# Block products' sums seeded in the accumulator banks instead of added from SBUF, in a hybrid three-branch trunk

## The chip, the core and the metric

The kernel runs on one core of a Trainium2 chip. The metric is device microseconds from the start to the end of the program; smaller is better. The profile names the engines PE (TensorE matmuls), PEld (TensorE weight loads), DVE (VectorE), ACT (ScalarE), POOL (GpSimd) and SP (SyncE, which issues most of the DMAs). "L452" is line 452 of the kernel's file.

## What is computed

A decoder trunk of two layers over 256 tokens of width 2048. Each layer normalises its input, projects it with one wide matrix into everything that three token mixers need (sparse attention, a convolution module, stick-breaking attention), and adds the gated sum of the three, projected once more, to its input:

```python
def hybrid_layer(x, norm_w, w_in, conv_w, conv_b, cln_w, cln_b, w_a_out, w_b_out, w_c_out, w_out, cos, sin, top_k):
    h = rms_norm(x, norm_w)
    proj = h @ w_in
    (qa, ka, va, za, qi, ki, wi, ub, zb, qc, kc, vc, zc, gates) = jnp.split(proj, split_points(), axis=-1)
    ...
    y_a = (dsa_attention(qa, ka, va, qi, ki, wi, top_k) * jax.nn.silu(za)) @ w_a_out
    y_b = (conformer_conv(ub, conv_w, conv_b, cln_w, cln_b) * jax.nn.silu(zb)) @ w_b_out
    y_c = (stick_breaking_attention(qc, kc, vc) * jax.nn.silu(zc)) @ w_c_out
    g = jax.nn.sigmoid(gates).reshape(b, s, N_BRANCH, D_MODEL)
    merged = g[:, :, 0] * y_a + g[:, :, 1] * y_b + g[:, :, 2] * y_c
    return x + merged @ w_out
```

All arrays are float32. The change concerns the merge gates of the second and third branch (`g[:, :, 1]`, `g[:, :, 2]`, each 2048 columns of `proj`) and half of the output projection `merged @ w_out`.

## The kernel before

**Products.** Weights come from HBM in units of 256 rows by 512 columns (512 KB), one DMA each on SP's queue. A unit is split into a rounded part (`wh`, or `ph`), made by an ACT cast at line 254, and a remainder (`wl`, `pl`), made by a DVE subtraction at line 258. The activations are split likewise, and each product is the sum of three: part by part, remainder by part, part by remainder. One matmul takes 128 rows and 512 columns; for one unit and one block of 128 tokens that is six matmuls, four with `wh` and two with `wl`, all recorded at line 268.

**The stage.** After the first branch, `run` (from line 520 on) works off one list of units per layer: the remaining gate columns, the branch projections and the output projection. It loads a unit 7 places ahead, casts and subtracts it 3 places ahead, issues its matmuls, and runs the unit's `now` actions behind them. `wh` and `wl` have three buffers each, and every fourth unit uses a buffer of its own (`ph`, `pl`). DVE and SP keep the order of the program; a scheduler places the rows of PE and ACT.

**Block products.** `seven` (from line 439 on) takes a pair of 512-column chunks and half of the 16 row blocks. Tokens, rows and columns are halved, and in place of eight block products it does seven, on sums of blocks of the weights (built by DVE, or by accumulating DMAs of POOL) and of the activations (`hs`, `sums`). There are five pairs in a layer: four of gate chunks, `(b, j)` = (2,0), (2,2), (1,0), (1,2), and one of the output projection. Each pair has four accumulator banks, called X and W (the two token blocks of one chunk) and Z and Y (of the other). The products run in the order P1, P7, P5, P6, P3, P2, P4, each as two half units; the `woven` list places these halves between the ordinary units by a position each, and `fetches` says at which unit the blocks that stay in SBUF are loaded. The other half of the rows is done by ordinary units (`gs`, and for the projection `stretch`), which add to the same banks. A bank's first matmul clears it; the function `opens` records which one that is.

**Sums of products.** Some products belong to more than one of the four results. Before, ACT copies P1 out of X (line 512) and DVE makes three combinations of it with Y and Z while these banks still grow (`combine`, line 452, four instructions per pair), in SBUF (`keep`): U1, U2 and R5. When the ordinary units have finished a bank, its combination is added: for gates in the function `gates` (line 1431) ahead of the sigmoid (line 1433), for the output projection in `arrive`, by the second addition (line 1508) behind that of the residual (line 1506). In layer 0, `leave` then squares the new residual and passes it on through `turned` to the next layer: DVE transposes (line 297), a store by POOL (line 300), a load back (line 306), and a scaling on DVE (line 666).

Four accumulator banks serve the pairs (`bk`, one tile each, taken anew by every pair), and four more, as two double tiles, serve the ordinary products (`acc`).

## Time and profile before

| | |
|---|---|
| median of 3 runs | 1995.35 us (1995.05 to 1995.38) |
| profiled execution | 1996.11 us |
| span of its profile | 1994.3 us |
| mean granted TensorE clock | 0.999 |
| DMA traffic | 472.19 MB, mean 237 GB/s |
| q1, hardware DMA queue | 389.25 MB, 61.5% of 16 engines' time |

The span runs from the first to the last instruction in the profile; the execution's own time has 1.81 us around it. In the chain of work that ended last, PE has 96%, DVE, DMA and issue 1% each. The profile gives one page of totals, and its trace can be asked for waits (who waited for whom, how long and how often), groups of equal instructions, windows of time, and the instructions of a stretch one after the other. In a timeline row the first number is the start in us, the second the duration; `x4` joins four like instructions that follow each other, and what stands in brackets is the idle time of that engine before it, with what ended it.

### The profile page before, as it was taken

Reading aid. Unit: us, or ns where it says so; the run is one execution under the profiler, and the core shown is the slowest. Engines: PE = TensorE matmul, PEld = TensorE weight load, DVE = VectorE, ACT = ScalarE, POOL = GpSimd, SP = SyncE. Lnnn points to the kernel's source line nnn. Section 1 sums busy time; section 2 is a strip of 40 time slices with the busy share of each in tenths; the row PEclk is TensorE's granted clock in tenths of the full one; section 3 lists DMA queues with packets and bytes.
Section 4 is the critical chain, followed back from the end, with each engine's and each line's share of the span. In section 5 each row is a group of like instructions: output and inputs, shape, how many; then the busy total and the mean of one; then the engine's idle time right before and its main releaser. Section 6 shows DMA issues by size and latency. Waiting matters only on the chain.

```text
span 1994.3 us, 26127 instructions
## 1 busy us (share of the span) xinstructions
PE 1983.5 (99%) x9266; PEld 1665.3 (84%) x9266; DVE 1643.4 (82%) x1855; ACT 1335.3 (67%) x1815; POOL 219.8 (11%) x324
## 2 busy tenths in 40 slices
PE   9999999999999999999999999999999999999998
PEld 8889888888888888888888988888888888888886
DVE  8767998878898878798785789988788978788997
ACT  7656667779866555565566576677888675555654
POOL 0111012100011100022111111121000110001120
PEclk9999999999999999999999999999999999999999
DMA  7788679866577887888977886788566778888994
GB/s 275 233 285 259 186 226 286 247 190 186 169 217 225 254 257 227 244 258 275 301 253 230 280 257 178 237 285 249 173 179 182 221 225 254 244 250 246 274 292 162
DMA packets 239938, 472.19 MB, mean 237 GB/s; under 512 B 17536, under 2 KB 30336, under 8 KB 239680
## 3 DMA queue, kind: packets, MB, share of 16 engines
q1 hardware_dynamic: 208768, 389.25, 61.5%
q0 software_dynamic: 29376, 78.14, 15.4%
q10 hardware_dynamic: 1664, 3.15, 0.4%
q8 instruction: 72, 1.18, 0.2%
q14 instruction: 58, 0.48, 0.1%
HBM read 437.70 MB, written 32.77 MB: 236 GB/s over the span
## 4 chain that ended last, share of the span: by engine, by line
PE 96%; DVE 1%; DMA 1%; issue 1%; POOL 0%; ACT 0%; DVEq 0%; POOLq 0%; ACTq 0%
PE acc L268 71%; PE bk L268 19%; PE mm L268 3%; DMA zy<-z 1%; PE mm L1089 1%; DVE wl L258 1%; PE mm L1180 0%; DMA z<-zt 0%; PE mm L1286 0%; PE mm L1232 0%; PE mm L1148 0%; DMA raw<-in_w_c_dram 0%; POOL z L300 0%; PE mm L844 0%; PE mm L1262 0%
## 5 line engine op out<-in xcount | busy, mean ns | idle before, releaser
L268 PE MATMUL acc<-wh,s 128*128 128x512 f32 (+1 forms) x4152 | 1028.0, 389 | 1.3 <-DVE s L1376 1.3
L258 DVE TENSOR_TENSOR wl<-raw,wh 128x1024 fp32r<-128x1024 f32 (+1 forms) x636 | 769.6, 1213 | 224.6 <-ACT wh L254 220.6
L254 ACT CAST wh<-raw 128x1024 fp32r<-128x1024 f32 (+1 forms) x635 | 660.9, 1044 | 377.7 <-PE acc L268 223.8
L268 PEld LDWEIGHTS acc<-wh,s 128*128 128x128 f32 x4152 | 772.1, 188 | 152.8 <-issue 2.0
L268 PE MATMUL acc<-wl,s 128*128 128x512 f32 (+1 forms) x1884 | 500.9, 388 | 0.6 <-DVE wl L258 0.6
L268 PEld LDWEIGHTS acc<-wl,s 128*128 128x128 f32 x1884 | 353.2, 188 | 72.0 <-DVE wl L258 1.0
L652 ACT ACTIVATE s<-yT,cst 128x256 f32<-128x256 f32 x480 | 209.7, 500 | 44.6 <-DVE s L929 43.6
L268 PE MATMUL bk<-wh,s 128*128 128x512 f32 x896 | 230.5, 389 | 0.0
L300 POOL DMA_DIRECT2D z<-zt x180 | 106.0, 602 | 1038.9 <-DVE zt L297 1037.9
L268 PEld LDWEIGHTS bk<-wh,s 128*128 128x128 f32 x896 | 167.9, 188 | 35.5 <-DVE t L452 0.9
L929 DVE TENSOR_TENSOR s<-s,s 128x1024 f32<-128x1024 f32 x120 | 146.3, 1219 | 0.0
L268 PE MATMUL bk<-wl,s 128*128 128x512 f32 x448 | 128.7, 389 | 0.0
L254 ACT CAST wh<-s 128x1024 fp32r<-128x1024 f32 x63 | 66.3, 1053 | 50.0 <-PE bk L268 24.2
L268 PEld LDWEIGHTS bk<-wl,s 128*128 128x128 f32 x448 | 84.1, 188 | 17.5
L258 DVE TENSOR_TENSOR wl<-s,wh 128x1024 fp32r<-128x1024 f32 x63 | 76.9, 1221 | 19.7 <-ACT wh L254 19.0
L268 PE MATMUL bk<-ph,s 128*128 128x512 f32 x304 | 78.5, 389 | 0.0
L496 POOL DMA_DIRECT2D s<-in_w_in_dram x32 | 38.7, 1209 | 323.0 <-DVE wl L258 149.6
L254 ACT CAST ph<-raw 128x1024 fp32r<-128x1024 f32 x47 | 49.5, 1054 | 32.7 <-PE bk L268 23.0
L268 PEld LDWEIGHTS mm<-s,wl 128*128 128x128 f32 x512 | 66.9, 191 | 5.0
L268 PEld LDWEIGHTS bk<-ph,s 128*128 128x128 f32 x304 | 57.1, 188 | 11.9
L306 POOL DMA_DIRECT2D zy<-z x50 | 36.5, 730 | 268.9 <-DMA z<-zt 79.6
L268 PE MATMUL mm<-s,wl 128*128 128x192 f32 x512 | 66.0, 271 | 0.0
(297 smaller groups left out, 1611.6 us busy)
## 6 DMA issues: line engine op xcount, KB each, us to landing
raw<-in_w_in_dram SPq DMA_DIRECT2D x519, 512.0 KB, 4.4
raw<-in_w_out_dram SPq DMA_DIRECT2D x56, 512.0 KB, 6.2
zy<-z POOLq DMA_DIRECT2D x48, 512.0 KB, 5.4
z<-zt POOLq DMA_DIRECT2D x172, 128.0 KB, 4.3
raw<-in_w_a_dram SPq DMA_DIRECT2D x32, 512.0 KB, 3.8
raw<-in_w_c_dram SPq DMA_DIRECT2D x32, 512.0 KB, 5.7
s<-in_w_in_dram POOLq DMA_DIRECT2D x32, 512.0 KB, 6.7
raw<-in_w_b_dram SPq DMA_DIRECT2D x32, 512.0 KB, 5.9
```

Of the source, the lines that this page charges most:

```text
L254: newest_parts[0] = nc.scalar.copy(u[1], u[0])
L258: newest_parts[1] = sub = nc.vector.tensor_sub(u[2], u[0], u[1].bitcast(F32))
L268: newest[0] = nc.tensor.matmul(o, lhsT, rhs, start=start, stop=stop, skip_group_check=True)
L300: nc.gpsimd.dma_start(z[:, :, :, a, :].rearrange("t b c e -> c (t b) e"), tmp[a * 32:(a + 1) * 32].rearrange("c t b k i -> c (t b) (k i)"))
L306: nc.gpsimd.dma_start(y.rearrange("p (t a) k i -> p t (a k i)", a=4), z.rearrange("t b c a e -> (b c) t (a e)"))
L496: nc.gpsimd.dma_start(held[to, h], block(b, h), accum_op=ALU.add)
L652: nc.scalar.activation(dst[:, i, :], y, AF.Copy, scale=wq)
L929: nc.vector.tensor_add(cs, cs, home(q - 1))
L1089: nc.tensor.matmul(ps[:, q * S:(q + 1) * S], qi[i][:, hd, :], ki[j][:, 0, :], start=n == 0, stop=n == 2)
```

## The change

The combinations are no longer kept in SBUF and added last. They are written into the banks ahead of the products that come later, and those products then accumulate on top. The products' order becomes P1, P2, P5, P6, P7, P3, P4. After P1, ACT copies X to SBUF (`save`); after P5, ACT copies Z, and DVE writes Z less the saved X into Y (`seed`); after P6, ACT copies Y into Z; after P7, DVE writes the saved Z less Y into W. For the pairs with `b == 2` that last difference goes to SBUF (`apart`) and is added ahead of one sigmoid as before. All other sigmoids read the banks, and `arrive` has one addition left. A bank that is seeded counts as opened. In the first pair of a layer an extra matmul opens Y (`fresh`). `banks` hands out the four tiles turned by two from pair to pair, so that X and W of a pair are Z and Y of the one before. The positions in `woven` and `fetches` are new, and so is where the gate units stand among the branch projections (`m`).

```diff
     def halves(tiles):
         return [v[:, i * 512:(i + 1) * 512] for v in tiles for i in range(2)]
-    def quarters(v):
-        v = v.rearrange("p (k a) t -> p k (a t)", a=2)
-        return [v[:, i, :] for i in range(4)]
     def forms(v):
         (a11, a12), (a21, a22) = ([v[:, i * 4:i * 4 + 4, t * P:(t + 1) * P] for i in range(2)] for t in range(NT))
...
         nc.vector.tensor_sub(a11, a11, a22)
         nc.vector.tensor_sub(a12, a12, a11)
-    def seven(w, cols, act, sums, banks, keep, by_transfer, long=()):
+    def seven(w, cols, act, sums, banks, keep, by_transfer, long=(), apart=None, fresh=False):
...
         X, W, Z, Y = range(4)
         held = {}
-        V, U2, U1, R5 = range(4)
-        def combine(op, dst, a, b):
-            dst, a, b = ({"b": banks, "k": keep}[n][0][i] for n, i in (dst, a, b))
-            op(dst, a, b)
+        def save(i, bank):
+            nc.scalar.copy(keep[0][i], banks[0][bank])
+        def seed(bank, a, b):
+            opens(banks[0][bank])
+            if b is None:
+                nc.scalar.copy(banks[0][bank], banks[0][a])
+            else:
+                nc.vector.tensor_sub(banks[0][bank], a(), b())
+        def bank_of(i):
+            return lambda: banks[0][i]
+        def kept(i):
+            return lambda: keep[0][i]
         def block(b, h):
             k, n = (int(i) - 1 for i in b)
...
             def products(u):
                 for i, j in ((0, 0), (1, 0), (0, 1)):
                     for k in range(2):
+                        if fresh and bank == X and opens(banks[0][Y]):
+                            mult(banks[0][Y], part(a, i, k0, 1, ts)[:, 0, :], u[1][:, 0, :], True, False)
                         mm = mult(banks[0][bank], part(a, i, k0 + h * 2 + k, 1, ts)[:, 0, :], u[1 + j][:, k, :],
                                   opens(banks[0][bank]), False)
                 return mm
...
         p1, p2, p4 = (("11", act, 0, 0, X), ("21", act, 4, 0, X), ("11", act, 4, 1, W))
         p5, p6, p3 = (("11", sums, 4, 1, Z), ("11", sums, 0, 0, Y), ("22", sums, 4, 0, Z))
         p7 = ("12", sums, 0, 1, Y)
-        order = [p1, p7, p5, p6, p3, p2, p4]
+        order = [p1, p2, p5, p6, p7, p3, p4]
         subs = [sub(h, *v) for v in order for h in range(2)]
-        P1, P7, P5, P6, P3, P2, P4 = (subs[n:n + 2] for n in range(0, 14, 2))
+        P1, P2, P5, P6, P7, P3, P4 = (subs[n:n + 2] for n in range(0, 14, 2))
         for h in range(2):
             for b, last, at in (("12", P1, P7), ("22", P5, P6), ("21", P6, P4)):
                 if b in by_transfer:
...
                 else:
                     at[h].early = [partial(add, h, "11", b)]
             P7[h].early = [*P7[h].early, partial(add, h, "12", "22")]
-        add_, sub_ = nc.vector.tensor_add, nc.vector.tensor_sub
-        P1[1].now = [lambda: nc.scalar.copy(keep[0][V], banks[0][X])]
-        P7[1].now = [partial(combine, add_, ("k", U1), ("k", V), ("b", Y))]
-        P5[1].now = [partial(combine, sub_, ("k", R5), ("b", Z), ("k", V))]
-        P6[1].now = [partial(combine, sub_, ("k", U1), ("b", Y), ("k", U1)),
-                     partial(combine, sub_, ("k", U2), ("k", V), ("b", Y))]
-        extra = {(0, 1): U2, (1, 0): U1, (1, 1): R5}
-        return fetch, subs, lambda q, t: keep[0][extra[q, t]] if (q, t) in extra else None
+        P1[1].now = [partial(save, 0, X)]
+        P5[1].now = [partial(save, 1, Z), partial(seed, Y, bank_of(Z), kept(0))]
+        P6[1].now = [partial(seed, Z, Y, None)]
+        if apart:
+            P7[1].now = [lambda: nc.vector.tensor_sub(apart(), keep[0][1], banks[0][Y])]
+        else:
+            P7[1].now = [partial(seed, W, kept(1), bank_of(Y))]
+        return fetch, subs
     def run(units, tasks):
...
         for i in (4, 0):
             split_at(hs, i, 4, v[:, i:i + 4, :])
+        turn = [0]
         def banks():
-            return Lazy(1, lambda: [mp[0].tile([P, 512], F32, tag="bk", name=nm("bk")) for _ in range(4)])
+            def make():
+                b = [mp[0].tile([P, 512], F32, tag="bk", name=nm("bk")) for _ in range(4)]
+                turn[0] += 2
+                return b[turn[0] % 4:] + b[:turn[0] % 4]
+            return Lazy(1, make)
         units, woven, fetches = [], [], []
         for b, j in ((2, 0), (2, 2), (1, 0), (1, 2)):
             og, act, wb = O_G + b * D, (gb, gc)[b - 1], (w_b, w_c)[b - 1][layer]
             g_banks, kept = banks(), Lazy(1, lambda: halves([t4(), t4()]))
-            fetch, subs, share = seven(w, (og + (j + 1) * 512, og + j * 512), hx, hs, g_banks, kept, ("12", "21"),
-                                       ("22",) if b == 2 else ())
+            fetch, subs = seven(w, (og + (j + 1) * 512, og + j * 512), hx, hs, g_banks, Lazy(1, lambda: [ev(), ev()]),
+                                ("12", "21"), ("22",) if b == 2 else (),
+                                (lambda kept=kept: kept[0][1]) if b == 2 else None, not units)
             base = len(units)
-            woven += [(base + (2.5 + 0.75 * n if b == 1 else 4.7 + 0.68 * n), u) for n, u in enumerate(subs)]
+            at, step = ((4.1, 0.64), (2.2, 0.8), (-0.3, 0.9), (-2.3, 1.14))[base // 16]
+            woven += [(base + at + step * n, u) for n, u in enumerate(subs)]
             ys, gs = [], []
             for q in (1, 0):
                 def g(q=q, g_banks=g_banks):
...
                 def sg(q=q, kept=kept):
                     return kept[0][q * 2:q * 2 + 2]
-                def gates(b, c, q, g, sg, share):
+                def gates(b, c, g, sg, apart):
                     for t in range(NT):
-                        v, to = g()[t], sg()[t]
-                        if share(q, t) is not None:
-                            nc.vector.tensor_add(to, v, share(q, t))
-                            v = to
-                        nc.scalar.activation(to, v, AF.Sigmoid)
+                        v = g()[t]
+                        if apart and t:
+                            nc.vector.tensor_add(sg()[t], v, sg()[t])
+                            v = sg()[t]
+                        nc.scalar.activation(sg()[t], v, AF.Sigmoid)
                     if b == 1 and c == 3:
                         warm_sqrt()
...
                 c, y = j + 1 - q, Lazy(1, token_accs)
                 gs += [plain(w, og + c * 512, hx, k, g, KD, True) for k in range(KC, KD, 2)]
                 ys.append([plain(wb, c * 512, act, k, partial(y.__getitem__, 0), KC) for k in range(0, KC, 2)])
-                gs[-1].now = [partial(gates, b, c, q, g, sg, share)]
+                gs[-1].now = [partial(gates, b, c, g, sg, b == 2 and not q)]
                 gs[-1].after = [partial(close, b, c, t, y, sg) for t in reversed(range(NT))]
             if j == 0:
                 ys = [[*ys[0][:2], *ys[1][:2]], [*ys[0][2:], *ys[1][2:]]]
                 if b == 1:
                     ys[0][-1].now = [settle]
-            m = 4 + b
+            m = 4 if b == 1 else 6
             units += ys[0] + ys[1] + gs[4:m] + gs[:4] + gs[m:]
-            fetches.append((fetch, (base - 2, base + 1) if b == 1 else (base + 4, base + 6)))
+            fetches.append((fetch, ((4, 6), (17, 19), (28, 31), (42, 45))[base // 16]))
         last = layer == DEPTH - 1
         ssq = small(8).rearrange("p (t j) -> p t j", t=NT)
...
         wo = w_out[layer]
         p0 = 0 if last else 2
         o_banks = banks()
-        fetch, subs, part_of = seven(wo, (p0 * 512 + 512, p0 * 512), mx, sums, o_banks, Lazy(1, lambda: quarters(slot())),
-                                     ("12", "21"))
+        fetch, subs = seven(wo, (p0 * 512 + 512, p0 * 512), mx, sums, o_banks, Lazy(1, lambda: [ev(), ev()]), ("12", "21"))
         acc, xcs, base = {}, {}, len(units)
         def accs(q):
...
             xc = xcs[q]
             for t in range(NT):
                 nc.vector.tensor_add(xc[:, t, :], acc[q][t], xc[:, t, :])
-                if part_of(p0 + 1 - q, t) is not None:
-                    nc.vector.tensor_add(xc[:, t, :], xc[:, t, :], part_of(p0 + 1 - q, t))
         def leave(q):
             xc, c0 = xcs[q], q * 512
```

In rows of the built program's order, a tile has its name and numbers, then what it is made from, the shape, and how many alike follow. Three places matter below.

**P1 to P2, second pair of layer 0.** On PE, where `bk` is a bank of the pair, `acc` a bank of the ordinary products and `s8` the activations; before:

```order
L268 MATMUL bk_1129_6509<-wh_1110_6407,s8_3_87 128x512 x4
L268 MATMUL bk_1129_6509<-wl_1111_6408,s8_3_87 128x512 x2
L268 MATMUL acc_1126_6491<-wh_1114_6429,s8_814_4854 128x512 x8
L268 MATMUL acc_1126_6491<-wl_1115_6430,s8_814_4854 128x512 x4
L268 MATMUL bk_1132_6512<-ph_1117_6447,s8_993_5871 128x512 x4
```

Here P1's second half ends in bank 6509, and P7 follows in another bank, 6512. Now:

```order
L268 MATMUL bk_1124_6472<-ph_1107_6368,s8_3_87 128x512 x4
L268 MATMUL bk_1124_6472<-pl_1108_6369,s8_3_87 128x512 x2
L268 MATMUL acc_1140_6529<-wh_1112_6409,s8_813_4853 128x512 x6
L268 MATMUL bk_1124_6472<-wh_1109_6386,s8_4_88 128x512 x4
L268 MATMUL bk_1124_6472<-wl_1110_6387,s8_4_88 128x512 x2
```

P2 now goes into P1's bank, with six matmuls of an ordinary unit between the two. On ACT, the row that reads the bank in that gap, in the changed order:

```order
L254 CAST wh_1109_6386<-raw_1111_6388 128x1024
L254 CAST wh_1112_6409<-raw_1114_6411 128x1024
L254 CAST wh_1116_6431<-raw_1118_6433 128x1024
L254 CAST ph_1119_6449<-raw_1121_6451 128x1024
L445 COPY ev_1133_6510<-bk_1124_6472 128x512
```

The save stands behind the cast of `ph_1119`.

**P7 to the gate unit, same pair.** On PE before, with P7 already past and P6's bank 6512 followed by other products:

```order
L268 MATMUL bk_1132_6512<-ph_1145_6579,s8_993_5871 128x512 x4
L268 MATMUL bk_1132_6512<-pl_1146_6580,s8_993_5871 128x512 x2
L268 MATMUL bk_1131_6511<-wh_1147_6590,s8_5_89 128x512 x4
L268 MATMUL bk_1131_6511<-wl_1148_6591,s8_5_89 128x512 x2
L268 MATMUL bk_1131_6511<-wh_1150_6609,s8_994_5872 128x512
L268 MATMUL bk_1132_6512<-wh_1147_6590,s8_5_89 128x512 x4
```

Now P7 is what ends in Y (6475), and an ordinary gate unit writes Z (6474) and Y by turns:

```order
L268 MATMUL bk_1127_6475<-wh_1152_6603,s8_993_5871 128x512 x4
L268 MATMUL bk_1127_6475<-wl_1153_6604,s8_993_5871 128x512 x2
L268 MATMUL bk_1126_6474<-wh_1155_6618,s8_5_89 128x512 x4
L268 MATMUL bk_1127_6475<-wh_1155_6618,s8_5_89 128x512 x4
L268 MATMUL bk_1126_6474<-wl_1156_6619,s8_5_89 128x512 x2
```

On DVE, the reads of these banks and what stands around them, before:

```order
L258 TENSOR_TENSOR wl_1151_6610<-long_1113_6426,wh_1150_6609 128x1024
L258 TENSOR_TENSOR wl_1153_6621<-long_1113_6426,wh_1152_6620 128x1024
L452 TENSOR_TENSOR t4_1139_6549<-bk_1132_6512,t4_1139_6549 128x512
L452 TENSOR_TENSOR t4_1138_6548<-t4_1138_6548,bk_1132_6512 128x512
L258 TENSOR_TENSOR pl_1155_6638<-raw_1156_6639,ph_1154_6637 128x1024
```

and now:

```order
L258 TENSOR_TENSOR wl_1156_6619<-raw_1157_6620,wh_1155_6618 128x1024
L258 TENSOR_TENSOR pl_1159_6638<-long_1103_6343,ph_1158_6637 128x1024
L258 TENSOR_TENSOR wl_1161_6648<-raw_1162_6649,wh_1160_6647 128x1024
L523 TENSOR_TENSOR t4_1173_6718<-ev_1134_6511,bk_1127_6475 128x512
L258 TENSOR_TENSOR wl_1164_6662<-long_1103_6343,wh_1163_6661 128x1024
```

Two reads of a bank have become one, with four matmuls between P7's last row and the next write of its bank.

**The end of layer 0's output projection.** On DVE, the rows of `arrive` (`t4` is the residual) and the transposes behind them, before:

```order
L1506 TENSOR_TENSOR t4_1468_8263<-bk_1409_7951,t4_1468_8263 128x512
L1508 TENSOR_TENSOR t4_1468_8263<-t4_1468_8263,s8_1416_7987 128x512
L1506 TENSOR_TENSOR t4_1468_8263<-bk_1410_7952,t4_1468_8263 128x512
L1508 TENSOR_TENSOR t4_1468_8263<-t4_1468_8263,s8_1416_7987 128x512
L258 TENSOR_TENSOR wl_1501_8416<-raw_1502_8417,wh_1500_8415 128x1024
L297 STREAM_TRANSPOSE zt_1507_8497<-t4_1468_8263 128x4x4x32
```

and now:

```order
L1523 TENSOR_TENSOR t4_1477_8262<-bk_1415_7947,t4_1477_8262 128x512
L1523 TENSOR_TENSOR t4_1477_8262<-bk_1416_7948,t4_1477_8262 128x512
L258 TENSOR_TENSOR wl_1510_8416<-raw_1511_8417,wh_1509_8415 128x1024
L297 STREAM_TRANSPOSE zt_1516_8495<-t4_1477_8262 128x4x4x32 x2
L258 TENSOR_TENSOR wl_1533_8577<-raw_1531_8574,wh_1532_8576 128x1024
```

Two additions are gone ahead of these transposes; a third goes with the other chunk of the pair.

## The prediction

> **What bounds the kernel now.** I read the busy shares first, then what TensorE (PE) waits for, then single stretches in order of time. In the profile page's first part each entry is busy time, share of the span, and instructions:
>
> ```profile
> PE 1983.5 (99%) x9266; PEld 1665.3 (84%) x9266; DVE 1643.4 (82%) x1855; ACT 1335.3 (67%) x1815; POOL 219.8 (11%) x324
> ```
>
> PE is busy for all but 10.8 us of the 1994.3-us span. The view of waits (total us, times, longest) lists everything that PE waited for in the whole run, and then, from the view of the weight loads (PEld), the one line that belongs to the code that changes:
>
> ```profile
> PE acc L268 <- DVE s L1376: 1.3, 1, 1.3
> PE mm L844 <- DVE eps L87: 1.1, 1, 1.1
> PE acc L268 <- DVE wl L258: 0.6, 1, 0.6
> ...
> PEld bk L268 <- DVE t L452: 0.9, 4, 0.2
> ```
>
> That is 3.0 us in three waits. Line 844 is the start of the program, line 1376 the passage ahead of the first block pair; both lie ahead of what changes. So the time is the number of matmuls times their pace, and an edit on another engine counts only through PE. The pace, from the timeline (start, duration, engine, line, operation):
>
> ```profile
> 975.90 1.98 PE L268 MATMUL bk<-wh,s 128*128 128x512 f32 x8
> 977.71 1.07 PE L268 MATMUL bk<-wl,s 128*128 128x512 f32 x4
> 978.62 0.39 PE L268 MATMUL bk<-ph,s 128*128 128x512 f32 x1
> ```
>
> Twelve matmuls take 978.62 − 975.90 = 2.72 us, 0.2267 each. To see how much the changed stage loses today I set its length against this pace:
>
> ```profile
> 675.15 1.07 PE L268 MATMUL bk<-wh,s 128*128 128x512 f32 x4
> ...
> 996.30 1.07 PE L268 MATMUL acc<-wh,s 128*128 128x512 f32 x4
> ```
>
> Between these two rows layer 0 issues 1416 matmuls of this form: 1416 × 0.22667 = 320.96 us, and 321.15 passed. The whole stage, pairs and all, loses 0.19 us. **There is nothing there to win**; what the change can do is lose, or alter the few waits elsewhere. The windows (busy time of each engine with its instructions, then granted clock and DMA share) show how near the other engines are: the first pair, and the stretch from the end of the gates into the output projection.
>
> ```profile
> core 0: us, PE busy (x) PEld busy (x) DVE busy (x) ACT busy (x) POOL busy (x), PEclk, DMA share, GB/s
> 667.00:733.00 66.00, 66.00 (x291) 54.50 (x292) 54.22 (x54) 38.21 (x39) 5.98 (x5) 1.00 0.88 272
> 912.00:986.00 74.00, 74.00 (x328) 61.29 (x327) 57.55 (x60) 41.67 (x49) 15.38 (x21) 1.00 0.94 287
> ```
>
> VectorE (DVE) is busy 82% in the first, ScalarE (ACT) 58%. Both have room on average, so what matters is when each single hand-off comes.
>
> **The change, part by part.** The additions that go and those that come have these durations (groups by shape: busy us, mean ns, idle before and its releaser):
>
> ```profile
> L258 DVE TENSOR_TENSOR wl<-raw,wh 128x1024 fp32r<-128x1024 f32 x83 | 100.9, 1220 | 23.4 <-ACT wh L254 22.5
> L254 ACT CAST wh<-raw 128x1024 fp32r<-128x1024 f32 x83 | 87.3, 1053 | 66.8 <-PE bk L268 37.9 <-PE acc L268 15.6 <-DVE raw L470 5.6
> L1379 DVE TENSOR_TENSOR s<-s,t 128x512 f32<-128x512 f32 x16 | 11.1, 692 | 0.6
> ...
> L452 DVE TENSOR_TENSOR t<-bk,t 128x512 f32<-128x512 f32 x8 | 5.5, 687 | 0.0
> ...
> L512 ACT COPY t<-bk 128x512 f32<-128x512 f32 x4 | 2.3, 578 | 0.0
> ```
>
> *Removed adds.* DVE has 46 additions fewer in both layers, 46 × 0.69 = 32 us of its 1643; ACT has 20 copies more, 20 × 0.58 = 12 us of its 1335. PE waited for neither there, so this counts nothing by itself; what hides it is PE's own stream of 321 us per layer.
>
> *Added matmuls.* In the first pair of each layer one extra product opens bank Y. 2 × 0.2267 = **+0.45 us**, straight on the bound engine.
>
> *The four old hand-offs.* Before, PE met DVE's additions at line 452 four times. One of them:
>
> ```profile
> 699.83 0.69 DVE L452 TENSOR_TENSOR t<-bk,t 128x512 f32<-128x512 f32 x1
> 700.43 0.68 DVE L452 TENSOR_TENSOR t<-t,bk 128x512 f32<-128x512 f32 x1
> ...
> 701.16 0.75 PEld L268 LDWEIGHTS bk<-wh,s 128*128 128x128 f32 x4 [0.21 <-DVE t L452]
> 701.21 1.15 PE L268 MATMUL bk<-wh,s 128*128 128x512 f32 x4
> ...
> 702.20 0.62 PE L268 MATMUL bk<-wl,s 128*128 128x512 f32 x2
> ```
>
> The weight load waits 0.21, yet the four matmuls take 702.20 − 701.21 = 0.99 instead of 0.91: 0.08 us lost. Four of these go: **−0.32 us**.
>
> *New hand-offs.* Now a sum must be *in the bank* before the next product of that bank starts, a wait that PE did not have. I counted in the changed order how many matmuls stand between the last product that feeds a sum and the first that needs the bank. P1 to P2 (ACT saves X): 6 in the second pair of a layer, 12 in the others. P5 to P6 (DVE seeds Y): 9 or more. P6 to the next writing of Y (ACT seeds Z from Y): 6 in the fourth pair, 12 or more elsewhere. P7 to the gate product that writes Y again (DVE reads Y): 7, 4, 5, 7 in the first four pairs, many in the last. What each needs: the two additions above follow each other without a pause, so the start costs some 0.05 and the release of PE another 0.05 (701.16 against the addition's end at 700.43 + 0.68 = 701.11), with 0.69 between them: 0.79 us on DVE, 0.68 on ACT. Cover: 4 matmuls are 0.91 us, 5 are 1.13, 6 are 1.36, 7 are 1.59. An idle engine always makes it. Two conditions remain. In the second pair ACT's save stands behind a cast of 1.05 us whose buffer comes free some 0.45 us before P1 ends, so 1.05 − 0.45 + 0.68 = 1.28 of 1.36: just hidden. And the eight with 4 to 7 matmuls stand behind a weight subtraction of 1.22 us on DVE. In the second pair its cast's buffer comes free 10 matmuls (2.27 us) before P7's end, cast and subtraction take 1.05 + 1.22 and two starts of 0.05, 2.37 together: it ends 0.10 us after P7, where 0.91 − 0.79 = 0.12 is what the cover leaves. I charge each of the eight what the old ones lost, 8 × 0.08 = **+0.64 us**. The ends: nothing at all, or a subtraction that has just begun each time, 1.22 + 0.79 = 2.01 us against the cover: 2 × (2.01 − 0.91) + 2 × (2.01 − 1.13) + 4 × (2.01 − 1.59) = 5.64 us for both layers. I stay near the low end, since the nearest row is the hand-off at 701.16.
>
> *Price of a write into a bank.* No row of before has DVE or ACT writing a bank. It is bounded by the nearest rows, below by nothing, above by the operation of twice the width: 1.22 us in place of 0.69 would leave the 4- and 5-matmul covers short by 2 × (1.32 − 0.91) + 2 × (1.32 − 1.13) = 1.20 us, and 1.05 in place of 0.58 on ACT leaves even the 6-matmul gap of the fourth pair covered (1.15 of 1.36). I take the price of a read, 0.69 and 0.58, whose rows have the same width. A page of the Trainium skill bears on this, "Perfetto Trace Analysis", section "Optimizing Scalar/DVE Operations": it gives VectorE some 60 ns of fixed overhead on SBUF and 125 on PSUM. By the groups above DVE's addition with a bank operand takes 687 against 692 without one, so the trace does not show it for reads, and no run here shows it yet for writes; by the page, 0.065 more on each seed would use half of the 0.12 us that the tightest cover leaves, and the sum would stay.
>
> *The layer change.* The third wait above, 0.6 us, hangs on the end of layer 0's output projection. The additions that go there, the chain behind them and the stall:
>
> ```profile
> L1508 DVE TENSOR_TENSOR t<-t,s 128x512 f32<-128x512 f32 x3 | 2.1, 692 | 0.1
> ...
> 1004.40 1.31 DVE zt L297 x2
> ...
> 1007.73 6.31 DMA z<-zt
> ...
> 1014.56 5.43 DMA zy<-z
> ...
> 1020.01 1.23 DVE L666 TENSOR_TENSOR s<-zy,cst 128x1024 f32<-128x1024 f32 x1 [3.18 <-DMA zy<-z]
> ...
> 1022.36 1.22 DVE L258 TENSOR_TENSOR wl<-raw,wh 128x1024 fp32r<-128x1024 f32 x1
> ...
> 1023.63 1.21 PE L268 MATMUL acc<-wl,s 128*128 128x512 f32 x4 [0.59 <-DVE wl L258]
> ```
>
> Transposes, store, load and scaling run as one chain; the scaling holds DVE's weight subtraction to 1022.36 and PE stands 0.59 us for it. In the changed order three additions of line 1508 (2.1 us) no longer stand ahead of these transposes, so the chain comes up to 2.1 us earlier, and 0.59 is all there is to win: **−0.59 us**. If the two DMAs take the gain, it is 0. What is late next is nothing that PE waits for in the page.
>
> *Order, banks, fetches.* The rotation gives the next pair's first banks to the tiles that the last pair left first; the gaps I counted there are 26 matmuls (5.9 us) or more, so releasing costs nothing, and it would cost only if a 0.6-us sigmoid came 5 us late. Transfers keep their number; fetches start at other units. The waits on their landing are ACT's, and one stands near PE:
>
> ```profile
> 931.27 1.05 ACT L254 CAST wh<-raw 128x1024 fp32r<-128x1024 f32 x1 [5.17 <-DMA raw<-in_w_out_dram]
> ...
> 933.74 1.07 PE L268 MATMUL acc<-wh,s 128*128 128x512 f32 x4
> ```
>
> Here the weights were 5.17 us late for ACT; the cast ended at 932.32 and PE took it at 933.74, 1.42 us to spare. I cost this at nothing, since the loads issue in the same order.
>
> **Sum**: 0.45 − 0.32 + 0.64 − 0.59 = +0.18 us. The profiled execution took 1996.11 us (1.81 around the span), 0.76 above the median of 1995.35; since all terms are differences I put them on the median: **1995.5 us**. Its own range goes from 1994.5 (stage losses of 0.36 in both layers and the old and layer-change waits gone, no new ones: 0.45 − 0.36 − 0.32 − 0.59 = −0.82) to 1996.7 (the price bound, 0.18 + 1.20).
>
> **Rivals.**
> 1. *Late seeds (slower).* Each of the eight short hand-offs meets DVE inside a subtraction of 1.22 us. For it: DVE runs in program order, is 82% busy, and the changed order puts a subtraction right ahead of the bank's read; my margin in the second pair is 0.02 us. Against it: the four old hand-offs, squeezed likewise, cost 0.08 each. It decides from the point where that subtraction ends more than 0.12 us after P7. Time: 1995.5 + 5.64 = 2001.1 us. Chance 0.07.
> 2. *Weights late.* The moved fetches push the load at 931.27 back by another 5.17 us: 5.17 − 1.42 = 3.75 us of PE, 1999.3. For it: DMA share 0.94 there. Against: the same bytes in the same queue. Chance 0.05.
> 3. *The layer change keeps its wait*, because the DMAs set it or another subtraction comes first; then that part of the change does nothing: 0.45 − 0.32 + 0.64 = +0.77, 1996.1. For it: 6.31 and 5.43 us of landing against 2.1 us of gain. Chance 0.14.
> 4. *The clock gate.* PE would idle briefly at each new hand-off and fall to half clock: 12 matmuls in 5.44 us instead of 2.72, once for each of the eight short hand-offs, 8 × 2.72 = 21.8 us, 2017.3. Against it, this stall and what followed:
>
> ```profile
> 666.88 2.08 PE L268 MATMUL acc<-wh,s 128*128 128x512 f32 x8 [1.25 <-DVE s L1376]
> ...
> 668.80 1.07 PE L268 MATMUL acc<-wl,s 128*128 128x512 f32 x4
> ```
>
> After 1.25 us of standing still the next 8 matmuls took 1.92 us against 1.81, and the window that begins there has a granted clock of 1.00. Chance 0.01. The rule stands in the Trainium skill, "TensorE: Matmul & The Clock Gate", section "A second HAM failure mode: psum-queue depth-cycling": short idle times between groups that cycle through accumulator banks make the clock fall and rise; by that rule, the trace of before does not agree, as far as its one longer gap shows.
>
> **How the numbers follow.** A measurement of this kernel tells about 0.2% from no change, 4.0 us: the bounds are 1991.4 and 1999.3. The forecast has 0.72, rival 1 0.07, rival 2 0.05, rival 3 0.14, rival 4 0.01, and 0.01 stays for a gain that nothing in the page shows, since all waits of PE together are 3.0 us. Slower: rivals 1 and 4 and, as 1999.3 lies on the bound, half of rival 2: 0.10. Faster: 0.01. Same: 0.89. The range goes from 1994.5 to rival 2's 1999.3, which leaves out rivals 1 and 4 and little more; the late seeds' full bound lies beyond it, the first half of it inside.
>
> **What would show it.** PE's matmuls number two more. In the waits of PE, line 258 is gone and line 1376 still has 1.3 us; weight loads of the banks wait for the seeds (lines 452 and 523 of the changed kernel) some 0.2 us each, about eight times. If a matmul into a bank shows half a microsecond or more behind these lines, rival 1 holds; if PE waits for a cast that waited for a load, rival 2; if 0.6 us remain near 1023, rival 3; a granted clock below 0.99 in a pair is rival 4. The forecast is wrong if the stage's 1416 matmuls and one take over 323 us.

## The result and the profile after

| | before | changed |
|---|---|---|
| median | 1995.2 us (4 runs, 1995.03 to 1995.38) | 2008.47 us (4 runs, 2006.95 to 2009.28) |
| ratio | | 1.0066, 95% interval 1.0048 to 1.0083 |
| profiled execution, span | 1996.11, 1994.3 | 2009.09, 2007.3 |
| mean granted clock | 0.999 | 0.997 |

The change makes the kernel slower by 13 us, 0.66%. The time lies outside the predicted range and on the side that had a chance of 0.10. The first part of the changed kernel's page, then everything that its PE waited for:

```profile
PE 1990.4 (99%) x9268; PEld 1666.3 (83%) x9268; DVE 1615.3 (80%) x1809; ACT 1341.8 (67%) x1835; POOL 219.4 (11%) x324
```

```profile
PE bk L268 <- DVE bk L452: 6.8, 3, 4.1
PE mm L852 <- DVE eps L87: 1.1, 1, 1.1
PE acc L268 <- DVE s L1384: 0.8, 1, 0.8
PE bk L268 <- ACT wh L254: 0.3, 1, 0.3
```

PE has two matmuls more, as forecast. DVE has 28 us of work less (forecast: 32), ACT 6.5 us more (forecast: 12). But PE, which before never stood at a bank of the pairs, now stands 6.8 us for the seed of a bank (line 452), in three places. Starts of the same matmuls in both traces show where the time came from:

| | before | changed | moved by |
|---|---|---|---|
| start of the stage, layer 0 | 666.88 | 666.16 | −0.72 |
| first matmul behind layer 0's last bank | 996.30 | 998.03 | +2.45 since the row above |
| start of the stage, layer 1 | 1656.81 | 1657.62 | −0.92 |
| tail behind layer 1's last bank | 1975.32 | 1988.34 | +12.21 |

That is 13.02 us. The layer change did win what was forecast, and somewhat more: its wait for line 258, 0.59 us, is gone from the list; where the rest of the 0.92 us comes from is not shown. Nearly all of the loss is in the second layer's stage. There PE stands twice, at the seeds of Y in the fourth and in the last pair. In the timeline, the rows behind each stall:

```profile
1865.16 1.87 PE L268 MATMUL bk<-ph,s 128*128 128x512 f32 x4 [2.09 <-DVE bk L452]
...
1867.69 2.53 PE L268 MATMUL acc<-wh,s 128*128 128x512 f32 x8
...
1870.06 1.07 PE L268 MATMUL acc<-wl,s 128*128 128x512 f32 x4
...
1940.14 1.78 PE L268 MATMUL bk<-ph,s 128*128 128x512 f32 x4 [4.06 <-DVE bk L452]
```

From 1865.16 to 1870.06 PE issues 14 matmuls, which take 4.90 us instead of 14 × 0.2267 = 3.17. The windows (clock in the column ahead of the DMA share) say why:

```profile
core 0: us, PE busy (x) PEld busy (x) DVE busy (x) ACT busy (x) POOL busy (x), PEclk, DMA share, GB/s
1865.00:1867.00 2.00, 1.84 (x5) 1.45 (x6) 2.00 (x3) 0.32 (x1) 0.20 (x1) 0.61 1.07 196
1867.00:1869.00 2.00, 2.00 (x7) 1.58 (x6) 1.95 (x3) 1.04 (x1) 0.99 (x1) 0.54 1.04 362
1869.00:1871.00 2.00, 2.00 (x11) 1.64 (x10) 1.92 (x2) 0.70 (x1) 0.00 (x0) 1.00 1.04 248
...
1940.00:1942.00 2.00, 1.86 (x5) 1.54 (x6) 2.00 (x3) 0.43 (x1) 0.48 (x1) 0.63 0.94 288
```

So each long stall costs 1.7 us again, at about half the clock. Of the 12.21 us, 2.09 + 4.06 + 0.27 are stalls, 2 × 1.73 the slow clock, 0.23 the extra product, and 2.1 are left: about 1.5 for the short hand-offs, 0.1 to 0.2 each, and 0.6 because weights of the last pair's P5 came late themselves.

Why the last seed was late stands in DVE's timeline. The products of P5, whose bank the seed reads, were done at 1933.3, and DVE, in order, works without a pause at what stands ahead:

```profile
1931.30 1.23 DVE L258 TENSOR_TENSOR wl<-s,wh 128x1024 fp32r<-128x1024 f32 x1 [6.51 <-ACT wh L254]
1932.44 1.22 DVE L476 TENSOR_TENSOR s<-s,s 128x1024 f32<-128x1024 f32 x1
1933.57 1.22 DVE L258 TENSOR_TENSOR wl<-raw,wh 128x1024 fp32r<-128x1024 f32 x1
1934.85 1.23 DVE L258 TENSOR_TENSOR pl<-s,ph 128x1024 fp32r<-128x1024 f32 x1
1935.99 1.22 DVE L599 TENSOR_TENSOR s<-zy,s 128x1024 fp32r<-128x1024 f32 x1
1937.13 1.22 DVE L476 TENSOR_TENSOR s<-s,s 128x1024 f32<-128x1024 f32 x1
1938.26 1.22 DVE L258 TENSOR_TENSOR wl<-raw,wh 128x1024 fp32r<-128x1024 f32 x1
1939.40 0.69 DVE L452 TENSOR_TENSOR bk<-bk,ev 128x512 f32<-128x512 f32 x1
```

Seven operations, 8.1 us, stand ahead of the seed. The first is the remainder of P5's own weights, the six behind it are for later units. All are late because the first had waited 6.51 us for an ACT cast. That cast waited for an accumulating load of weight blocks. The chain that ended last has it (11.10 us to land), and POOL's timeline says when it was issued:

```profile
1917.72 0.72 POOL L306 DMA_DIRECT2D zy<-z  x1 [8.45 <-DMA z<-zt]
1918.42 0.60 POOL L300 DMA_DIRECT2D z<-t  x1
1919.02 1.26 POOL L504 DMA_DIRECT2D s<-in_w_out_dram  x1
```

```profile
1919.02 11.10 DMA s<-in_w_out_dram
...
1930.21 1.06 ACT wh L254
```

The load stood in POOL's queue behind a load-back that waited 8.45 us for its store. Before, POOL had the two the other way round:

```profile
1909.29 1.24 POOL L496 DMA_DIRECT2D s<-in_w_out_dram  x1 [0.53 <-DVE wl L258]
1910.67 0.72 POOL L306 DMA_DIRECT2D zy<-z  x1
```

In the fourth pair the seed is late by the same road but a smaller cause: ACT stands 2.85 us for a load-back that line 598 scales, and DVE has five operations between its scaling (1856.81) and the seed (1864.41).

### The profile page after: what moved, and what is told of

It reads as the page before. It is cut to its first block, busy times and chain, and to the rows that moved or that the text cites. A ratio compares the mean times of both kernels' runs of the same rounds, so it can differ in the third digit from the quotient of the medians.

```text
span 2007.3 us, 26101 instructions
## 1 busy us (share of the span) xinstructions
PE 1990.4 (99%) x9268; PEld 1666.3 (83%) x9268; DVE 1615.3 (80%) x1809; ACT 1341.8 (67%) x1835; POOL 219.4 (11%) x324
## 4 chain that ended last, share of the span: by engine, by line
PE 94%; DMA 2%; DVE 2%; issue 1%; ACT 1%; POOL 0%; DVEq 0%; ACTq 0%; POOLq 0%
PE acc L268 69%; PE bk L268 19%; PE mm L268 3%; DMA zy<-z 1%; DMA z<-zt 1%; PE mm L1097 1%; DMA s<-in_w_out_dram 1%; DVE wl L258 0%; PE mm L1188 0%; DVE s L476 0%; PE mm L1294 0%; PE mm L1240 0%; PE mm L1156 0%; DVE s L599 0%; PE mm L852 0%
## 5 line engine op out<-in xcount | busy, mean ns | idle before, releaser
L258 DVE TENSOR_TENSOR wl<-raw,wh 128x1024 fp32r<-128x1024 f32 (+1 forms) x630 | 761.9, 1212 | 228.3 <-ACT wh L254 224.7
L268 PE MATMUL bk<-wh,s 128*128 128x512 f32 x905 | 235.4, 391 | 0.9 <-DVE bk L452 0.6
L254 ACT CAST wh<-s 128x1024 fp32r<-128x1024 f32 x71 | 74.6, 1052 | 69.5 <-PE bk L268 51.1
L258 DVE TENSOR_TENSOR wl<-s,wh 128x1024 fp32r<-128x1024 f32 x71 | 86.5, 1220 | 33.7 <-ACT wh L254 33.4
L254 ACT CAST ph<-raw 128x1024 fp32r<-128x1024 f32 x53 | 55.8, 1053 | 49.9 <-PE bk L268 25.2
L258 DVE TENSOR_TENSOR pl<-raw,ph 128x1024 fp32r<-128x1024 f32 x53 | 64.7, 1221 | 14.3 <-ACT ph L254 11.6
```

The lines of the kernel that those rows point to most:

```text
L254: newest_parts[0] = nc.scalar.copy(u[1], u[0])
L258: newest_parts[1] = sub = nc.vector.tensor_sub(u[2], u[0], u[1].bitcast(F32))
L268: newest[0] = nc.tensor.matmul(o, lhsT, rhs, start=start, stop=stop, skip_group_check=True)
```

## The experiments

The theory from these rows, A: DVE and ACT work in order, and fall behind by some us whenever a transfer is late. Before, this was free, because a combination had no deadline. Now a product waits for it. The rival, B: the new places of products and fetches starve the weights, and PE would wait whoever adds the sums.

**1. The old sums in the new places.** Before's kernel with three edits:

```diff
-            woven += [(base + (2.5 + 0.75 * n if b == 1 else 4.7 + 0.68 * n), u) for n, u in enumerate(subs)]
+            at, step = ((4.1, 0.64), (2.2, 0.8), (-0.3, 0.9), (-2.3, 1.14))[base // 16]
+            woven += [(base + at + step * n, u) for n, u in enumerate(subs)]
...
-            m = 4 + b
+            m = 4 if b == 1 else 6
...
-            fetches.append((fetch, (base - 2, base + 1) if b == 1 else (base + 4, base + 6)))
+            fetches.append((fetch, ((4, 6), (17, 19), (28, 31), (42, 45))[base // 16]))
```

> Old sums (combined in SBUF, added last, old product order, no turning of the banks) with the new positions of products, fetches and gate units. Theory A (the seed of Y after P5 is a deadline that the in-order queues of DVE and ACT miss in two pairs of the second layer, and the clock falls after those stalls): no seed, no deadline, 1995.5 us, within 1.5. Theory B (the new positions starve the weights, and PE waits whoever adds the sums): 2004 us or more, with PE waiting for casts or loads in the pairs.

Measured: 1996.85 us against 1996.41 of before in the same runs, ratio 1.0000 (0.9990 to 1.0009). B falls. ACT's timeline, and the waits of PE, show that the lateness itself is there as well:

```profile
1921.66 1.05 ACT L254 CAST wh<-s 128x1024 fp32r<-128x1024 f32 x1 [4.65 <-DMA s<-in_w_out_dram]
```

```profile
PE acc L268 <- DVE s L1376: 1.3, 1, 1.3
PE mm L844 <- DVE eps L87: 1.1, 1, 1.1
PE acc L268 <- DVE wl L258: 0.4, 1, 0.4
PE acc L268 <- ACT ph L254: 0.2, 1, 0.2
```

The same load makes ACT wait 4.65 us at the same place, and no product of a bank waits for anything. The new places make the engines late; it takes the rest of the change to make PE pay. That rest is the seeds together with the new order of products and the turned banks, which this kernel leaves out as well; experiment 10 separates them.

**2. One deadline less.**

```diff
-        P5[1].now = [partial(save, 1, Z), partial(seed, Y, bank_of(Z), kept(0))]
+        P5[1].now = [partial(save, 1, Z)]
```

> The changed kernel without the one subtraction that seeds Y after P5 (its result leaves out that term; P6 then starts Y by itself). A: the waits of PE for it (0.61, 2.09 and 4.06 us) and the two slow stretches behind the longer ones (some 1.7 us each) go: 2008.5 - 6.8 - 3.5 = 1998.2 us, within 1.5. B: 2006 us or more, the stalls stay in the same places with another releaser.

Measured: 2009.05 us, ratio 1.0058 (1.0042 to 1.0075): no gain. A's number was wrong. The timeline shows where the stalls went:

```profile
887.93 1.19 PE L268 MATMUL bk<-wh,s 128*128 128x512 f32 x4 [2.40 <-DVE bk L452]
...
1882.79 2.08 PE L268 MATMUL bk<-wh,s 128*128 128x512 f32 x4 [2.02 <-DVE bk L452]
...
1949.60 1.20 PE L268 MATMUL bk<-ph,s 128*128 128x512 f32 x4 [2.31 <-ACT bk L450]
```

They moved to the next hand-offs of the same pairs: the seed of W after P7, the copy into Z after P6. I read this so: PE's stall at the first deadline is what lets DVE and ACT catch up; without it they stay late and the next deadline collects. A then says that the lag of the queues is what costs, wherever the next deadline stands.

**3. More room between P5 and P6.** In the fourth pairs and the last one of the second layer:

```diff
-            woven += [(base + at + step * n, u) for n, u in enumerate(subs)]
+            woven += [(base + (5.05 + 0.55 * (n - 6) if base == 48 and n in (6, 7) else at + step * n), u)
+                      for n, u in enumerate(subs)]
...
-            woven += [(base + 1.2 + 0.9 * n, u) for n, u in enumerate(subs)]
+            woven += [(base + (7.05 + 0.6 * (n - 6) if n > 5 and n < 10 else 1.2 + 0.9 * n), u)
+                      for n, u in enumerate(subs)]
```

> P6 later by half a unit in the fourth pair of both layers and in the last pair of the second, so that 24 instead of 12 matmuls lie between P5 and P6 there; sums as in the changed kernel. A: the stall of 2.09 us goes, that of 4.06 shrinks by 2.7 to 1.3 and with them the slow stretches: 2008.5 - 2.1 - 2.7 - 3.5 = 2000.2 us, within 2. B: no gain, 2007 or more, since late weights stay as late.

Measured: 2003.41 us, 1.0035 (1.0023 to 1.0047). It gains, but 3 us less than expected. The last pair's 4.06 became 1.22, as worked out; stalls of 0.57, 0.81 and 1.39 us came at the copies into Z, as in experiment 2. No slow clock is left (0.999 for the run).

**4. The last pair half a unit earlier,** so that POOL issues the load first:

```diff
-            woven += [(base + 1.2 + 0.9 * n, u) for n, u in enumerate(subs)]
+            woven += [(base + 0.7 + 0.9 * n, u) for n, u in enumerate(subs)]
```

> The last pair of the second layer starts half a unit earlier; nothing else. By the order, POOL then issues the second half of the block's accumulating load ahead of the load-back of the merged gate, not behind it. Theory A1 (the 4.06-us stall comes from that load, which was issued at 1919.02 behind a load-back that waited 8.45 us): the load lands some 6 us earlier, the stall, its slow stretch and the 0.27 us go: 2008.5 - 4.1 - 1.7 - 0.3 = 2002.4 us, within 1.5; the 2.09-us stall of the pair before stays. Theory A2 (the load takes long in itself since the queues are full): the stall stays above 3 us, 2007 or more.

Measured: 2002.6 us, 1.0031 (1.0021 to 1.0041). POOL's and ACT's timelines:

```profile
1912.12 1.21 POOL L504 DMA_DIRECT2D s<-in_w_out_dram  x1 [3.61 <-ACT wh L254]
1917.59 0.73 POOL L306 DMA_DIRECT2D zy<-z  x1 [4.27 <-DMA z<-zt]
```

```profile
1924.20 1.05 ACT L254 CAST wh<-s 128x1024 fp32r<-128x1024 f32 x1 [0.76 <-PE bk L268]
```

Issued at 1912.12, the load no longer holds ACT, and the stall of the last pair is gone. A1 holds. That the time came out as expected is in part luck: in the fourth pair of the second layer the stall shrank from 2.09 to 1.62 us and its slow stretch went too, which A1 did not have, while in other places a stall of 0.61 grew to 0.90 and stalls of 0.84 and 0.36 us came.

**5. The seed ahead of the save.** In the first layer of the changed kernel, the groups show five seeds with 4.8 us of idle time ahead of them, which ended with ACT's copy of the same bank:

```profile
L452 DVE TENSOR_TENSOR bk<-bk,ev 128x512 f32<-128x512 f32 x5 | 3.5, 699 | 4.8 <-ACT ev L445 4.8
```

```diff
-        P5[1].now = [partial(save, 1, Z), partial(seed, Y, bank_of(Z), kept(0))]
+        P5[1].now = [partial(seed, Y, bank_of(Z), kept(0)), partial(save, 1, Z)]
```

> The changed kernel with two statements behind P5 in the other order: DVE seeds Y first, ACT saves Z second. In the changed kernel each seed of Y begins only when ACT's copy of the same bank has ended (idle 0.54 us for it). Theory C (the two reads of one bank are put in a row, so the hand-off needs 0.6 us more than its own operation): the wait for the save goes, the stalls of 0.61 and 2.09 us lose 0.6 us each or go, the 4.06 stays within 0.7 (DVE itself is late there): 2008.5 - 1 to 2 = 2007 us. Theory D (ACT's queue is what is late): the stalls change by over 1 us each.

Measured: 2010.03 us, 1.0075 (1.0060 to 1.0090), against 1.0066 of the changed kernel: the same. The order turned round as C has it, and ACT now waits for DVE:

```profile
1865.62 0.59 ACT L445 COPY ev<-bk 128x512 f32<-128x512 f32 x1 [0.61 <-DVE bk L452]
```

The stall of 2.09 shrank to 0.28, more than C allows; that of 0.61 went, and that of 4.06 stayed, at 4.19, both as C has it. Stalls of 1.42 and 1.08 came at the next seeds: experiment 2 again. A further one of 2.14 us, in the first pair of the second layer, followed a cast that waited 3.43 us for another accumulating load. The Trainium skill, "PSUM — Partial Sum Buffer", section "PSUM bank collisions raise a hardware error", says that a scheduler orders any two engines' accesses to one bank, two reads among them. By that rule, the trace agrees: the second read begins when the first has ended, and its engine has waited 0.54 us for that at the seed of the changed kernel's fourth pair (second layer), 0.61 us in the row above.

**6. The merged chunk used later,** on top of 4, against the lag in the fourth pair:

```diff
-                        turned([mg[c // 2][:, c % 2, t, :] for t in range(NT)], partial(use_m, c), LATER - (3, 1, -1, 3)[c],
+                        turned([mg[c // 2][:, c % 2, t, :] for t in range(NT)], partial(use_m, c), LATER - (1, 1, -1, 3)[c],
```

> The kernel with the earlier last pair, and the first merged chunk's scaled parts used two units later, so that neither ACT nor DVE stands for the load-back (2.85 us on ACT) just ahead of the fourth pair's P5. Theory A: with DVE and ACT no longer late there, the stalls of 0.9 and 1.62 us in the fourth pair shrink below 0.5: 2002.6 - 2.5 = 2000 us, within 1. If the fourth pair is late because its DVE work is too much in itself, the stalls stay and the time is 2002 or more.

Measured: 1999.44 us, 1.0018 (1.0009 to 1.0027). As A has it: two stalls at a bank are left, of 0.28 us each.

```profile
PE bk L268 <- DVE bk L452: 0.6, 2, 0.3
```

**7. The seed ahead of the weight preparation,** on the changed kernel:

```diff
+            urgent = u.size < 1 and u.now
+            if not urgent:
+                ahead(n)
             count[0] += u.size
-            run_tails(count[0])
+            if not urgent:
+                run_tails(count[0])
             mm = u.products(got.pop(n))
...
+            if urgent:
+                ahead(n)
+                run_tails(count[0])
...
```

> The changed kernel with the saves, seeds and products of a half unit that ends in a seed issued ahead of the weight preparation for the units behind it, so that DVE has one subtraction, and where there is one an addition of blocks, less ahead of each seed. Theory A (the seed stands in DVE's order behind work for later units): stalls shrink by 1.2 to 2.4 us each, 4.06 to 1.7 to 2.9, 2.09 to 0: 2008.5 - 1.2 - 2.1 - 0.6 - 1.7 = 2003 us, within 2. If what is late is the data of P5 itself, the stalls stay: 2007 or more.

Measured: 2003.37 us, 1.0040 (1.0025 to 1.0055). The 4.06 became 1.94, in the range given; no slow stretch followed it:

```profile
1936.21 1.21 PE L268 MATMUL bk<-ph,s 128*128 128x512 f32 x4 [1.94 <-DVE bk L452]
```

Five operations instead of seven stand ahead of this seed, and the stall is 2.12 us shorter. So the place in DVE's order counts, at about one operation's time for each place. Here too a lag went on to a later deadline: the fourth pair's stall of 2.09 us went, and one of 1.45 came at its seed of W.

**8. All four repairs together.**

> The earlier last pair, the later use of the merged chunk, the seed ahead of the save and ahead of the weight preparation, in one kernel. Theory A: no stall above 0.5 us is left, and what remains over the kernel before are two products (0.45 us) and some sixteen hand-offs of 0.1 to 0.2 us each: +2 us, 0.1% over the kernel before in the same runs, and not faster than it, since nothing that the change removes was on PE. If a term is missing from the account, it is 3 us or more over.

Measured: 1998.31 us against 1995.63, ratio 1.0015 (1.0006 to 1.0025), 3.0 us over. PE's stalls at banks are down to one of 0.42 us. The expectation was +2 us and named 3 us or more as the sign of a missing term; with an interval from 1.2 to 5.0 us the time does not decide it. Nor are the two repairs of experiments 5 and 7 seen to add anything to the 1.0018 of experiment 6. What is left are mostly short waits of the weight loads:

```profile
PEld bk L268 <- ACT bk L450: 1.9, 3, 0.8
PEld bk L268 <- DVE bk L452: 1.8, 6, 0.3
PEld bk L268 <- DVE t L523: 1.2, 4, 0.3
PEld bk L268 <- ACT ev L445: 0.5, 2, 0.2
```

**9. The seed of Y repeated** 5 to 13 times, on top of 8:

```diff
-        P5[1].now = [partial(seed, Y, bank_of(Z), kept(0)), partial(save, 1, Z)]
+        late[0] += 1
+        P5[1].now = [partial(seed, Y, bank_of(Z), kept(0))] * (1 + 4 + 2 * ((late[0] - 1) % 5)) + [partial(save, 1, Z)]
```

> The kernel of all four repairs, with the seed of Y written 5, 7, 9, 11 and 13 times over in the five pairs of each layer (the same values each time), so that DVE is late by a known amount. Theory A gives for each the stall of PE: 0.79 us and 0.6 more for each repetition, less the cover (9 matmuls, 2.04 us, in the first pair, 12, 2.72 us, elsewhere): 1.2, 1.7, 2.9, 4.1 and 5.3 us, twice, 30 us in all on top of 1998.3. On the clock: if its fall is set by the length of the stall, a line between 1.6 and 2.1 us separates stalls with and without a slow stretch; if not, equal stalls of the two layers will differ. A slow stretch costs 1.7 us: with six of them, 2038 us.

Measured: 2036.47 us, one run. The second pair of the first layer:

```profile
752.75 5.10 DVE L454 TENSOR_TENSOR bk<-bk,ev 128x512 f32<-128x512 f32 x7 [1.76 <-PE bk L268]
...
757.91 1.20 PE L268 MATMUL bk<-wh,s 128*128 128x512 f32 x4 [0.66 <-DVE bk L454]
```

A repetition takes 5.10 / 7 = 0.73 us, not 0.6. The stalls of PE are 0.66, 2.12, 3.59 and 5.06 us in pairs two to five of the first layer and 0.66, 2.13, 3.59 and 5.06 in the second; none in the first pairs. Each pair has two repetitions more, 1.46 us, and each stall is 1.46 to 1.47 us longer: once the cover is used up, lateness goes to PE one for one. The cover is 20 matmuls here and not 12, since the scheduler put eight matmuls of the next unit between as well; so my numbers came out too large, most so for the short stalls. That the total came near the 2038 us named is in part luck: the stalls came to 22.9 us and not 30, the slow clock to some 9 us, about as expected, and waits for weights that I had not counted filled part of the gap.

**10. No seeds at all,** in the kernel of experiment 8 (the terms are left out of the gates and of the output projection):

```diff
-        P5[1].now = [partial(seed, Y, bank_of(Z), kept(0)), partial(save, 1, Z)]
-        P6[1].now = [partial(seed, Z, Y, None)]
+        P5[1].now = [partial(save, 1, Z)]
         if apart:
-            P7[1].now = [lambda: nc.vector.tensor_sub(apart(), keep[0][1], banks[0][Y])]
-        else:
-            P7[1].now = [partial(seed, W, kept(1), bank_of(Y))]
+            P7[1].now = [lambda: nc.vector.tensor_copy(apart(), keep[0][1])]
```

> The kernel of all four repairs without the writes into banks (the seeds of Y, Z and W, and the read of Y in the pairs with a difference in SBUF; the results leave out these terms), everything else in its place. It measures what the hand-offs cost together where no queue is late: by the prediction's 0.08 us for each of eight 0.6 us; by the rows of the changed kernel, 0.12 to 0.2 us for each of some fourteen, 2 us, so 1996.3 against 1998.3 in the same runs. If nothing is gained, the rest over the kernel before is not in the hand-offs.

Measured: 1994.9 us against 1996.2 of before, ratio 0.9994 (0.9985 to 1.0003). Against experiment 8's 1.0015 that is 0.0021, some 4 us, with an uncertainty of about 2.6. The traces say the same, from the first matmul into a pair's bank to the one behind the last, in each layer: at 0.22667 us per matmul, experiment 8 loses 1.44 and 3.02 us there, this kernel 0.10 twice, the kernel before 0.19 and 0.16. So the seeds' hand-offs are what was left, and the new order of products and the turned banks, which this kernel keeps, cost nothing here.

## Why the prediction was wrong

- **What bounds the kernel, and that there is nothing to win**: right. PE stays 99% busy, and neither the changed kernel nor any of the ten experiments was clearly faster than before.
- **Extra matmuls, old hand-offs, layer change** (+0.45, −0.32, −0.59): right. PE has two matmuls more, the wait for line 258 is gone, and the way to layer 1 took 0.92 us less, which is more than the 0.59.
- **Price of a write into a bank**: right, 0.699 us for a seed, 0.577 for the copy, the price of a read.
- **New hand-offs**: the step that failed. "P5 to P6 (DVE seeds Y): 9 or more" was left out of the charge, since "an idle engine always makes it", and the upper bound, 5.64 us, let DVE be late by one subtraction, at the eight hand-offs with 4 to 7 matmuls alone. The runs show DVE late by seven operations, 8.1 us, behind one late transfer, and by five in the fourth pair: at P5 to P6, charged with nothing, stand 6.76 us of stalls and 3.5 us of slow clock behind them. The prediction itself says that the mean load does not settle this, but never asked how late DVE can be; the same trace had ACT waiting 5.17 us for a load at 931.27, which I priced only against PE's casts. The size of a short hand-off was off as well: I charged 0.08 us for eight, where the changed kernel has about 15 that lose 0.1 to 0.2 each. And it missed that ACT's save and DVE's seed of one bank follow each other.
- **Order, banks, fetches at nothing**: failed. I counted the transfers and wrote that "the loads issue in the same order", which does not hold in POOL's queue: one accumulating load had fallen behind a waiting load-back. Experiment 1 shows that this alone costs nothing, experiment 4 that with the seeds it is worth some 7 us (1.0066 against 1.0031).
- **Rivals**: "late seeds" had the right mechanism at the wrong hand-off, with a bound that was too low. "Weights late" had the right cause, but the way from there to PE led over the seeds. "The clock gate" was dismissed on one gap of 1.25 us; the clock did fall behind the gaps of 2.09 and 4.06 us, and 3.5 us of the loss is its doing. It was not the short hand-offs that brought it down.

## What to carry to other kernels

An operation that nobody waits for hides how late its engine runs. Before making PE wait for it, read how far the in-order queue falls behind after the worst late transfer, count all that stands ahead in that queue, and set this against the cover, not the operation's own duration. Such a lag is not cured at one hand-off, since the next one collects it: cure the transfer, or the place in the queue. And where loads share a queue with instructions that wait, compare their order, not their number.

## What the runs showed of the hardware

PE's granted clock fell to half behind eleven stalls of 2.02 us and more in the changed stages of these runs, and stayed behind all of 1.94 us and less. Each fall lasted 3.41 us, or 6.83 behind the stalls of 4.19 and 5.06 us, and lost PE 1.7 us for every 3.41 in which it had work. Around 2.1 us it went both ways. In experiment 9, the stall of 2.12 us in the first layer (up to 818.33) and that of 2.13 us in the second (up to 1828.05), in windows of 3.41 us:

```profile
816.01:819.42 3.41, 1.28 (x6) 0.90 (x6) 3.31 (x6) 0.59 (x1) 0.00 (x0) 1.00 0.00 0
819.42:822.83 3.41, 3.19 (x8) 2.08 (x7) 3.41 (x4) 3.04 (x3) 0.00 (x0) 0.50 0.32 79
822.83:826.24 3.41, 3.41 (x16) 2.65 (x15) 3.41 (x3) 1.29 (x2) 1.20 (x1) 1.00 1.07 384
1822.94:1826.35 3.41, 2.98 (x14) 2.13 (x12) 3.27 (x5) 0.00 (x0) 0.00 (x0) 1.00 0.61 110
1826.35:1829.76 3.41, 1.65 (x6) 1.05 (x6) 3.34 (x5) 1.12 (x2) 0.00 (x0) 1.00 0.00 0
1829.76:1833.17 3.41, 2.71 (x10) 1.72 (x10) 3.35 (x4) 2.19 (x3) 0.35 (x1) 1.00 0.52 157
```

The bounds of these windows are not chosen freely: within each trace, all changes of the granted clock stand whole multiples of 3.41 us apart (in the changed kernel, after the first fall at 1865.43: 1, 21, 1 and 17). The first stall lies within one window, of which PE stands idle 2.13 us, and the clock is at half for the next. The second is cut in two, 0.43 us before the bound at 1826.35 and 1.70 behind it, and the clock stays. Cut into such windows, the traces of all twelve kernels (before, changed, ten experiments) show a fall behind every full-clock window in which PE stands 1.90 us or more, and behind none in which it stands 1.76 us or less. So not the length of a stall decides, but how much of it falls into one window; where the bounds lie is chance. The Trainium skill, "TensorE: Matmul & The Clock Gate", section "What's actually happening", has a window of about 3.4 us that runs freely and looks at how busy PE was. By that rule, the trace agrees in the length of the window and in its running freely; but 1.90 us of idle time within one window was enough, where that page names about 3.4 us of it.
